# Shorter reciprocal square roots for every norm of a two-block fp32 kernel

## The chip, the cores and the metric

The kernel runs on one core of one Trainium2 chip, as one program. The metric is the device time of a run in microseconds; three runs of the kernel before are known. A further execution was taken by the hardware profiler, and every row shown here comes from that one.

## The reference

Two blocks in sequence, all in fp32, on 256 tokens of width 1024. The first has two layers; x (256 tokens) and a context xc (256 tokens, updated in layer 0 only) go through one set of weights:

```python
h = _rmsnorm(x, p["norm_g"]) * (1.0 + scale[:, None, :]) + shift[:, None, :]
hp = h @ p["w_in"]
...
y = jax.nn.silu(_layernorm(y, p["conv_ln_g"], p["conv_ln_b"]))
return y @ p["w_pw"] + p["b_pw"]
...
y = jnp.concatenate([attn, conv, four, sgu], axis=-1) * jax.nn.silu(hp[..., GATE_OFF:])
return y @ p["w_out"]
```

scale, shift and gate come from a product with w_ada. The attention has an rmsnorm on its query and key parts, the spatial gating (sgu) a layer norm. The result is rmsnorm(x, final_g). The second block has two layers of three steps, each with a norm before and behind it:

```python
x = x + 0.5 * rmsnorm(swiglu(rmsnorm(x, g[0]), ...), g[1])
x = x + rmsnorm(token_mixer(rmsnorm(x, g[2]), ...), g[3])
x = x + 0.5 * rmsnorm(swiglu(rmsnorm(x, g[4]), ...), g[5])
```

Each of these norms needs 1/sqrt of a mean square or variance for every token.

## The kernel before

Tokens lie on the 128 partitions: x is two tiles (t = 0, 1; x_80 and x_81 in the orders below), the context two more (t = 2, 3). An fp32 product is made as three fp32r products of high and low parts: ACT rounds a weight (`whi`, line 216 by its helper), DVE takes the rest (`wlo`, line 221), and PE runs whi*hi, whi*lo and wlo*hi (line 230; transposes are line 234). Weights and the chunks of w_ada come in over SP's queue as 512 KB tiles (`raw`, `ada`; line 330) into a few shared buffers, so that a fetch starts when an older tile has been consumed: a raw by its wlo on DVE, an ada chunk by its two `adaj` instructions on DVE, which multiply it with the condition and sum.

The order of all instructions is written when the program is built, by a planner (`Sched`). It keeps a clock for every engine, adds a cost for every instruction it issues (DVE: 0.07 us plus 0.00104 per element plus an extra; 0.13 between dependent instructions of one engine, 0.22 between engines), and starts side jobs, such as a conv's layer norm (`conv_out`), an ada chunk or a norm, when its clocks say that their inputs are there. A different cost anywhere can so change the order of everything behind it. The instruction streams themselves are static: an engine takes its instructions in that order, and waits where an input is late.

Stages of the first block, by layer: norm and modulation (`modulate`), the products with w_in (`u`), attention (`mla`), conv (31 `acc` steps per tile half on DVE), Fourier, sgu, the gate product (`u` of 256 columns), then for each branch `y` is multiplied (`fac`), transposed (`tpy`, into `yT`), and w_out is applied (`yo`), and x is updated. `conv_out` transposes acc (`tpc`), makes the layer norm from it (`bn`, `mv`, `rwl`, the root, `lnb`, then `ln` on ACT), transposes ln (`tpc` again), applies Silu or Tanh (`cs`, in layer 1 also `cv`), multiplies with w_pw (`pw`), and adds the row (`fac<-pw`). `norms` of the second block ends with x<-u_post,rs_y,x and the transposes of x for the next step (`tpx`).

The root is `rsqrt` (lines 372 to 386): a seed from the bits (rs_y, an integer operation on w), half of w negated (rs_h), then three steps y = (y*y*h + 1.5)*y. For width 1 a step is two instructions, for width 2 or 4 three. It is called by `rms` (norms, prenorm, the final norm; width 1), `modulate` (1), `layernorm` (1), `mla` (2, or 1 for keys alone), `attn_b` (4) and `First.start` (4).

Of the kernel before, what the change touches and what calls it, by code (L numbers as in the profile page):

```python
# [8 lines left out]
F32 = mybir.dt.float32  # L9
F32R = mybir.dt.float32r  # L10
I32 = mybir.dt.int32
AF = mybir.ActivationFunctionType
ALU = mybir.AluOpType
PSUM = bass.MemoryType.PSUM
P = 128
# [353 lines left out]

def rsqrt(S, ch, pool, w, n, tag):

    y = pool.tile([P, n], F32, tag=tag + "y", name="rs_y", bufs=4)
    h = pool.tile([P, n], F32, tag=tag + "h", name="rs_h")
    t = pool.tile([P, n], F32, tag=tag + "t", name="rs_t")
    S.dve(ch, n, "tensor_scalar", y.bitcast(I32), w.bitcast(I32), -0.5, float(0x5F3759DF), op0=ALU.mult, op1=ALU.add)
    S.dve(ch, n, "tensor_scalar", h, w, -0.5, None, op0=ALU.mult)
    for _ in range(3):
        if n == 1:  # L380
            S.dve(ch, n, "scalar_tensor_tensor", t, y, h, y, op0=ALU.mult, op1=ALU.mult, x=0.06)
        else:
            S.dve(ch, n, "tensor_tensor", t, y, y, op=ALU.mult)
            S.dve(ch, n, "tensor_tensor", t, t, h, op=ALU.mult)
        S.dve(ch, n, "scalar_tensor_tensor", y, t, 1.5, y, op0=ALU.add, op1=ALU.mult)
    return y


class Second:
# [57 lines left out]
    def rms(self, ch, ss, eps=D * EPS):  # L447

        w = self.small.tile([P, 1], F32, tag="rw", name="rw")
        self.S.dve(ch, 1, "scalar_tensor_tensor", w, ss[:, 0:1], eps, ss[:, 1:2], op0=ALU.add, op1=ALU.add)  # L450
        return rsqrt(self.S, ch, self.small, w, 1, "r")
# [413 lines left out]
    def attn_b(self, t, l, M, ev):  # L865
# [37 lines left out]
        for b in range(2):  # L903
# [7 lines left out]
        S.dve(ch, 256, "tensor_reduce", ss, sq, axis=mybir.AxisListType.X, op=ALU.add)  # L911
        S.dve(ch, 4, "tensor_scalar", ss, ss, 64 * EPS, None, op0=ALU.add)
        r = rsqrt(S, ch, small, ss, NB, "rb")
        S.dve(ch, 256, "scalar_tensor_tensor", o, o, 8.0 * (1.0 - LAM_INIT[l]), r.unsqueeze(2).to_broadcast([P, NB, 64]),
              op0=ALU.mult, op1=ALU.mult)
# [50 lines left out]
class First:  # L966
# [169 lines left out]
    def start(self):  # L1136
# [53 lines left out]
        w = self.small.tile([P, 4], F32, tag="rw4", name="rw4", bufs=1)  # L1190
        S.dve(cx, 4, "scalar_tensor_tensor", w, ss[:, :, 0], EPS, ss[:, :, 1], op0=ALU.add, op1=ALU.add)
        r = rsqrt(S, cx, self.small, w, 4, "r4")
        dg = [self.w2([P, P], f"diag{t}") for t in range(4)]
        for t in range(4):
# [662 lines left out]
def build(tc, a, wst, widths, n1, tab, ident, cols, rows, lamp, out):  # L1857
    nc = tc.nc
    with ExitStack() as ctx:
        def pool(name, bufs, **k):  # L1860
            return ctx.enter_context(tc.tile_pool(name=name, bufs=bufs, **k))


        pool("pad", 1).tile([P, PADS[0] // 4], F32, name="pad")
        wp, hp, work, rawp, cp = pool("wp", WBUFS), pool("hp", 2), pool("work", 2), pool("rawp", RAWB), pool("const", 1)
        small, psA = pool("small", 2), pool("psA", 1, space=PSUM)

        class PS:
            def tile(self, shape, dt, tag, name):
                return psA.tile(shape, dt, tag=tag, name=name, bufs={"ps": 6, "tp": 2}[tag])  # L1870

        X = [cp.tile([P, D], F32, name=f"x{t}") for t in range(2)]
        ones = cp.tile([P, P], F32, name="ones")
        nc.gpsimd.memset(ones, 1.0)
        idn = cp.tile([P, P], F32, name="ident")
        nc.gpsimd.dma_start(idn, ident)
        cl = cp.tile([P, cols.shape[1]], F32, name="cols")
        nc.gpsimd.dma_start(cl, cols)
        lp = cp.tile([P, 128], F32, name="subln")
        st = Stream(tc, wst, widths, rawp, wp, WBUFS, RAWB)  # L1880
        S = Sched(tc, st, LEAD)
        ps = PS()
        one = ExitStack()
        p1 = one.enter_context(tc.tile_pool(name="first", bufs=1, reuse_waits="tile"))
        first = First(tc, S, X, cl, idn, ones, ps, work, small, hp, p1, a, [0, n1 // 2])
        second = Second(tc, S, X, cl, rows, idn, lp, ones, out, ps, work, small, hp)
        first.end = second.first
        left = [0, 1]

        def main(t):  # L1890
            yield from first.main(t)
            left.remove(t)
            if not left:
                assert all(x[1].__name__ == "prenorm" for x in S.sides), S.sides
                one.close()
                p2 = ctx.enter_context(tc.tile_pool(name="second", bufs=1, reuse_waits="tile"))
                second.open(p2, tab)
                second.lambdas(lamp[:, :256])
                st.widen(st.alloc(p2, WMORE), WMORE)
                st.rawb = RAWB  # L1900
            yield from second.main(t)

        first.consts()
        S.spawn(first.start())
        st.widen(lambda i: [first.s4([P, 1024], f"w{n}{i}", F32R) for n in range(2)], WX[0], WX[1], WX[2])
        mains = {t: main(t) if t < 2 else first.main(t) for t in range(4)}
        nc.gpsimd.dma_start(lp, lamp[:, 256:].to_broadcast([P, 128]))
        S.run(mains)
# [37 lines left out]
```

## Time and profile before

| | us |
|---|---|
| median of three runs | 1448.87 (1445.61, 1448.87, 1448.91) |
| the profiled execution | 1447.77 |
| its span | 1446.0 |
| PE busy in the span | 1403.1 |
| DVE busy | 1002.7 |
| ACT busy | 765.8 |

The span runs from the first to the last recorded event of the profiled execution; the run's own time is 1.8 us longer. Busy times are of instructions and may overlap on an engine, since the next one can start before the last has ended. The first block takes from 0 to about 440 us, the second the rest.

### The profile page before, as it was taken

How to read it: one execution, taken by the hardware profiler on the slowest of the kernel's cores; microseconds unless marked ns; L12 is line 12 of the kernel's file. 1: busy time of each engine (PE TensorE's matmuls, PEld its weight loads, DVE VectorE, ACT ScalarE, POOL GpSimd, SP SyncE). 2: the span in 40 equal slices, each digit the busy share in tenths (PEclk: the TensorE clock that was granted, in tenths of full speed). 3: DMA queues.
4: the chain of work that ended last, by engine and by line, in shares of the span. 5: the costliest groups of instructions: out<-in, count | busy, mean ns of one | idle time of the engine just before them, and what ended most of it. 6: DMA issues, size and time to landing. Idle time of an engine off the chain costs nothing.

```text
span 1446.0 us, 19092 instructions
## 1 busy us (share of the span) xinstructions
PE 1403.1 (97%) x6766; PEld 1134.5 (78%) x6766; DVE 1002.7 (69%) x2175; ACT 765.8 (53%) x1348; POOL 30.0 (2%) x46
## 2 busy tenths in 40 slices
PE   7999997999999999999999999999999999999997
PEld 4778886777877888777878888788887778788886
DVE  4899978779787555587886555765555878865554
ACT  4465533576565444567655444554445676554442
POOL 1000000000000000000000000000000000000000
PEclk9999999999999999999999999999999999999999
DMA  8751455333456555653446566566566534466551
GB/s 304 238 172 59 128 192 162 123 124 121 159 189 209 186 188 188 190 186 121 139 139 204 189 180 186 173 193 187 188 189 189 182 125 134 143 200 186 185 186 58
DMA packets 69088, 245.64 MB, mean 170 GB/s; under 512 B 7841, under 2 KB 8097, under 8 KB 68865
## 3 DMA queue, kind: packets, MB, share of 16 engines
q1 hardware_dynamic: 66384, 235.11, 51.1%
q0 software_dynamic: 2176, 8.79, 1.8%
q8 instruction: 53, 0.87, 0.2%
q10 hardware_dynamic: 432, 0.53, 0.1%
q14 instruction: 43, 0.34, 0.1%
HBM read 243.35 MB, written 1.05 MB: 169 GB/s over the span
## 4 chain that ended last, share of the span: by engine, by line
PE 79%; DVE 11%; DMA 4%; ACT 3%; issue 2%; SPq 0%; DVEq 0%; ACTq 0%
PE u L230 37%; PE y L230 18%; PE m L230 9%; DMA raw<-in_wst_dram 3%; PE yo L230 3%; DVE adaj L221 2%; DVE wlo L221 2%; PE av L230 2%; PE tpg L234 2%; DVE acc L221 1%; ACT whi L216 1%; PE tpp L234 1%; DMA ada<-in_adan_dram 1%; PE sc L230 1%; ACT f L216 1%
## 5 line engine op out<-in xcount | busy, mean ns | idle before, releaser
L221 DVE TENSOR_TENSOR wlo<-raw,whi 128x1024 fp32r<-128x1024 f32 (+1 forms) x380 | 459.2, 1211 | 341.8 <-ACT whi L216 339.4
L216 ACT CAST whi<-raw 128x1024 fp32r<-128x1024 f32 (+1 forms) x380 | 395.3, 1042 | 386.7 <-PE u L230 228.5
L230 PE MATMUL u<-whi,h_hi 128*128 128x512 f32 x704 | 281.2, 400 | 1.1 <-ACT h_hi L216 1.1
L230 PE MATMUL u<-whi,h_lo 128*128 128x512 f32 x704 | 275.0, 391 | 0.6 <-DVE h_lo L221 0.6
L230 PE MATMUL u<-wlo,h_hi 128*128 128x512 f32 x704 | 275.5, 392 | 0.0
L230 PE MATMUL y<-whi,g 128*128 128x512 f32 x704 | 218.3, 390 | 0.5 <-ACT g L216 0.5
L230 PEld LDWEIGHTS y<-whi,g 128*128 128x128 f32 x704 | 132.0, 188 | 28.8 <-ACT g L216 0.8
L230 PEld LDWEIGHTS u<-wlo,h_hi 128*128 128x128 f32 x704 | 132.1, 188 | 27.7
L230 PEld LDWEIGHTS u<-whi,h_lo 128*128 128x128 f32 x704 | 132.5, 188 | 27.1 <-DVE h_lo L221 2.5
L230 PEld LDWEIGHTS u<-whi,h_hi 128*128 128x128 f32 x704 | 132.2, 188 | 26.4 <-ACT h_hi L216 1.7
L230 PE MATMUL y<-wlo,g 128*128 128x512 f32 x352 | 137.3, 390 | 0.0
L230 PE MATMUL u<-whi,hhi 128*128 128x512 f32 (+2 forms) x256 | 98.7, 388 | 0.4 <-ACT whi L216 0.3
L221 DVE CUSTOM_DVE_ANT_0 adaj<-ada,cbc 128x1024 bf16<-128x1024 f32 x76 | 90.6, 1221 | 8.7 <-DMA ada<-in_ada_dram 8.6
L230 PE MATMUL u<-wlo,hhi 128*128 128x512 f32 (+2 forms) x256 | 94.4, 372 | 0.4 <-DVE wlo L221 0.4
L230 PE MATMUL u<-whi,hlo 128*128 128x512 f32 (+2 forms) x256 | 94.8, 372 | 0.0
L230 PE MATMUL m<-whi,h_hi 128*128 128x512 f32 x192 | 79.0, 415 | 0.4 <-ACT h_hi L216 0.4
L230 PEld LDWEIGHTS y<-wlo,g 128*128 128x128 f32 x352 | 66.1, 188 | 14.3
L230 PE MATMUL m<-wlo,h_hi 128*128 128x512 f32 x192 | 75.5, 395 | 0.0
L230 PE MATMUL m<-whi,h_lo 128*128 128x512 f32 x192 | 75.3, 394 | 0.0
L221 DVE SCALAR_TENSOR_TENSOR acc<-glu,cw,acc 128x512 f32<-128x512 f32 (+1 forms) x120 | 70.8, 613 | 0.0
L230 PEld LDWEIGHTS u<-whi,hhi 128*128 128x128 f32 x256 | 48.2, 189 | 8.3 <-issue 1.9
L230 PEld LDWEIGHTS u<-wlo,hhi 128*128 128x128 f32 x256 | 48.2, 188 | 8.0 <-DVE wlo L221 1.2
(294 smaller groups left out, 1961.6 us busy)
## 6 DMA issues: line engine op xcount, KB each, us to landing
raw<-in_wst_dram SPq DMA_DIRECT2D x376, 512.0 KB, 3.6
ada<-in_ada_dram SPq DMA_DIRECT2D x42, 512.0 KB, 4.3
grow<-in_rows_dram POOLq DMA_DIRECT2D x10, 512.0 KB, 5.1
raw<-in_wst_dram SPq DMA_DIRECT2D x8, 416.0 KB, 3.1
ada<-in_adan_dram SPq DMA_DIRECT2D x6, 512.0 KB, 5.3
raw<-in_wst_dram SPq DMA_DIRECT2D x8, 256.0 KB, 2.8
tab<-in_tab_dram POOLq DMA_DIRECT2D x1, 1536.0 KB, 8.4
x<-in_x_dram SPq DMA_DIRECT2D x2, 512.0 KB, 5.4
```

Source lines behind the costliest of these rows:

```text
L216: ins = getattr(self.nc.scalar, fn)(*a, **k)
L221: ins = getattr(self.nc.vector, fn)(*a, **k)
L230: self.nc.tensor.matmul(*a, **k)
L234: self.nc.tensor.transpose(out, in_, ident)
```

## The change

`rsqrt` makes two steps instead of three: one of third order, y = ((t + H1)*t + H0)*y with t = y*w*y, and one of second order with scaled constants, y = (t + N0)*y. The seed's constant is another, the signs are folded into the constants, and h is not needed. For width 1 the instructions go from 8 to 6, for the others from 11 to 8. An assertion when the first block's buffers are closed allows one more kind of side job to be open.

```diff
@@ -369,20 +369,30 @@
+SEED, H1, H0, N0 = -552954042.0, -2.0555939659688196, 1.8980594831935855, -1.8898815769682833
 def rsqrt(S, ch, pool, w, n, tag):
     y = pool.tile([P, n], F32, tag=tag + "y", name="rs_y", bufs=4)
-    h = pool.tile([P, n], F32, tag=tag + "h", name="rs_h")
     t = pool.tile([P, n], F32, tag=tag + "t", name="rs_t")
-    S.dve(ch, n, "tensor_scalar", y.bitcast(I32), w.bitcast(I32), -0.5, float(0x5F3759DF), op0=ALU.mult, op1=ALU.add)
-    S.dve(ch, n, "tensor_scalar", h, w, -0.5, None, op0=ALU.mult)
-    for _ in range(3):
+    p = pool.tile([P, n], F32, tag=tag + "h", name="rs_p")
+    def square():
         if n == 1:
-            S.dve(ch, n, "scalar_tensor_tensor", t, y, h, y, op0=ALU.mult, op1=ALU.mult, x=0.06)
+            S.dve(ch, n, "scalar_tensor_tensor", t, y, w, y, op0=ALU.mult, op1=ALU.mult, x=0.06)
         else:
             S.dve(ch, n, "tensor_tensor", t, y, y, op=ALU.mult)
-            S.dve(ch, n, "tensor_tensor", t, t, h, op=ALU.mult)
-        S.dve(ch, n, "scalar_tensor_tensor", y, t, 1.5, y, op0=ALU.add, op1=ALU.mult)
+            S.dve(ch, n, "tensor_tensor", t, t, w, op=ALU.mult)
+    S.dve(ch, n, "tensor_scalar", y.bitcast(I32), w.bitcast(I32), -0.5, SEED, op0=ALU.mult, op1=ALU.add)
+    square()
+    S.dve(ch, n, "scalar_tensor_tensor", p, t, H1, t, op0=ALU.add, op1=ALU.mult)
+    S.dve(ch, n, "scalar_tensor_tensor", y, p, H0, y, op0=ALU.add, op1=ALU.mult)
+    square()
+    S.dve(ch, n, "scalar_tensor_tensor", y, t, N0, y, op0=ALU.add, op1=ALU.mult)
     return y
@@ -1891,7 +1901,7 @@
             yield from first.main(t)
             left.remove(t)
             if not left:
-                assert all(x[1].__name__ == "prenorm" for x in S.sides), S.sides
+                assert all(x[1].__name__ in ("prenorm", "swiglu") for x in S.sides), S.sides
                 one.close()
                 p2 = ctx.enter_context(tc.tile_pool(name="second", bufs=1, reuse_waits="tile"))
                 second.open(p2, tab)
```

The planner's costs of the root change with it, and so does the order. On DVE there are 2035 rows of the order before and 1910 now; the numbers of PE, ACT, POOL and SP instructions are the same, their order is not: about a thousand rows of PE move, nearly all in the first block.

PE, output stage of layer 0. u is the gate product's last part (its name has a number), tpc<-ident,acc and tpc<-ident,ln the conv's transposes, yo the product with w_out. Before:

```order
L234 MATMUL tpc<-ident,acc 128x128 x2
L230 MATMUL yo_2466<-whi_2259,yT_2281 128x512
L234 MATMUL tpc<-ident,acc 128x128 x2
L230 MATMUL yo_2466<-wlo_2260,yT_2280 128x512
L230 MATMUL yo_2466<-whi_2259,yT_2280 128x512
L230 MATMUL yo_2466<-whi_2259,yT_2281 128x512
L230 MATMUL yo_2466<-wlo_2260,yT_2280 128x512
L234 MATMUL tpc_2473<-ident,ln 128x128 x2
L234 MATMUL tpc_2491<-ident,ln 128x128 x2
L230 MATMUL pw<-pw,cs 128x256 x4
L234 MATMUL tpc_2521<-ident,ln 128x128 x2
L234 MATMUL tpc_2539<-ident,ln 128x128 x2
```

and now:

```order
L230 MATMUL u_2293<-wlo_2081,hhi 128x256
L234 MATMUL tpy<-ident,y_1417 128x128 x2
L234 MATMUL tpc_2345<-ident,ln 128x128 x2
L234 MATMUL tpc_2351<-ident,ln 128x128 x2
L230 MATMUL pw<-pw,cs 128x256 x4
L234 MATMUL tpc_2369<-ident,ln 128x128 x2
L234 MATMUL tpc_2381<-ident,ln 128x128 x2
L230 MATMUL pw<-pw,cs 128x256 x2
L234 MATMUL tpy<-ident,y_1226 128x128 x2
L230 MATMUL pw<-pw,cs 128x256 x2
L234 MATMUL tpy<-ident,y_1226 128x128 x4
L230 MATMUL yo_2410<-whi_2302,yT_1741 128x512
```

The conv's transposes of acc and ln and the pw product stood behind dozens of yo; now the transposes of acc stand further up, amid the gate product, and those of ln and the whole pw product stand between the gate product and the first yo.

DVE, the same place: ada_04 to ada_06 are chunks of w_ada of layer 1, y_1271 (before) and y_1226 (now) the branch that the transposes behind the gate product need. Before:

```order
L221 ISA adaj,ada_115<-ada_04_2112,cbc_117 128x1024
L221 ISA ada_115 128x1
L221 ISA adaj,ada_115<-ada_04_2112,cbc_118 128x1024
L221 ISA ada_115 128x1
L221 ISA adaj,ada_115<-ada_05_2142,cbc_117 128x1024
L221 ISA ada_115 128x1
L221 ISA adaj,ada_115<-ada_05_2142,cbc_118 128x1024
L221 ISA ada_115 128x1
L221 TENSOR_TENSOR y_1271<-y_1271,fac 128x256 x2
L221 TENSOR_TENSOR wlo_2236<-raw_2067,whi_2235 128x1024
L221 ISA adaj,ada_115<-ada_06_2165,cbc_117 128x1024
L221 ISA ada_115 128x1
```

and now:

```order
L221 SCALAR_TENSOR_TENSOR rs_y<-rs_t,rs_y 128x1 x2
L221 SCALAR_TENSOR_TENSOR lnb<-mv,rs_y 128x1 x2
L221 ISA adaj,ada_115<-ada_04_2095,cbc_117 128x1024
L221 ISA ada_115 128x1
L221 ISA adaj,ada_115<-ada_04_2095,cbc_118 128x1024
L221 ISA ada_115 128x1
L221 TENSOR_TENSOR yT_2020<-tpy,yT_2019 128x2x128
L221 ISA adaj,ada_115<-ada_05_2116,cbc_117 128x1024
L221 ISA ada_115 128x1
L221 ISA adaj,ada_115<-ada_05_2116,cbc_118 128x1024
L221 ISA ada_115 128x1
L221 TENSOR_TENSOR y_1226<-y_1226,fac 128x256 x2
```

Before, the conv's layer norms (rs_y, lnb) come some twenty rows behind ada_06; now they come ahead of ada_04, and ada_05 stands ahead of y, ada_06 behind its first pair.

PE, the boundary behind the first mixer of the second block: tpx transposes x_80 for the next unit, tpm transposes o_b, a part of the second token tile's attention. Before:

```order
L230 MATMUL y_1_7103<-whi_6952,m_hi 128x512
L230 MATMUL y_1_7103<-whi_6952,m_lo 128x512
L230 MATMUL y_1_7103<-wlo_6953,m_hi 128x512
L234 MATMUL tpm<-ident,o_b 128x128 x2
L234 MATMUL tpx<-ident,x_80 128x128 x4
L230 MATMUL y_0_7102<-whi_6979,m_hi 128x512
L230 MATMUL y_1_7103<-whi_6979,m_hi 128x512
L234 MATMUL tpx<-ident,x_80 128x128 x4
```

and now:

```order
L234 MATMUL tpm<-ident,o_b 128x128 x2
L230 MATMUL y_1_7027<-whi_6879,m_hi 128x512
L230 MATMUL y_1_7027<-whi_6879,m_lo 128x512
L230 MATMUL y_1_7027<-wlo_6880,m_hi 128x512
L230 MATMUL y_0_7026<-whi_6906,m_hi 128x512
L230 MATMUL y_1_7027<-whi_6906,m_hi 128x512
L234 MATMUL tpx<-ident,x_80 128x128 x8
```

The first four transposes of x_80 move two y matmuls down, to the other four; tpm moves three up.

## Rows read from the trace of the kernel before

**Rows 1.** The page's first part: busy time, share and instructions of each engine.

```profile
PE 1403.1 (97%) x6766; PEld 1134.5 (78%) x6766; DVE 1002.7 (69%) x2175; ACT 765.8 (53%) x1348; POOL 30.0 (2%) x46
```

**Rows 2.** Busy time by stretch; then PE's granted clock, DMA share, GB/s.

```profile
210.00:240.00 30.00, 26.46 (x147) 22.43 (x145) 25.06 (x64) 9.00 (x16) 0.31 (x1) 0.94 0.65 211
240.00:270.00 30.00, 25.61 (x120) 20.27 (x119) 21.39 (x58) 13.72 (x31) 0.00 (x0) 0.94 0.47 149
760.00:914.00 154.00, 154.00 (x694) 125.45 (x693) 83.21 (x97) 72.41 (x96) 0.00 (x0) 1.00 0.61 191
```

**Rows 3.** PE's waits: total us, times, longest us.

```profile
PE tpc L234 <- ACT ln L216: 4.0, 1, 4.0
PE tpx L234 <- DVE x L221: 4.0, 5, 0.9
PE tpy L234 <- DVE y L221: 3.5, 1, 3.5
...
PE tpy L234 <- ACT cv L216: 1.6, 1, 1.6
```

**Rows 4.** Instructions that write rs_y: ns min/median/max, first and last start, forms.

```profile
L221 DVE SCALAR_TENSOR_TENSOR rs_y<-rs_t,rs_y x165: 136/158/168, 14.4 to 1441.4; 128x1 f32<-128x1 f32 x132, 128x2 f32<-128x2 f32 x18, 128x4 f32<-128x4 f32 x15
```

**Rows 5.** Timeline of DVE, one root of width 1: start us, us, line.

```profile
269.95 0.15 DVE L221 TENSOR_SCALAR rs_y<-rw 128x1 int32<-128x1 int32 x1
270.02 0.14 DVE L221 TENSOR_SCALAR rs_h<-rw 128x1 f32<-128x1 f32 x1
270.20 0.22 DVE L221 SCALAR_TENSOR_TENSOR rs_t<-rs_y,rs_h 128x1 f32<-128x1 f32 x1
270.46 0.16 DVE L221 SCALAR_TENSOR_TENSOR rs_y<-rs_t,rs_y 128x1 f32<-128x1 f32 x1
...
271.55 0.49 DVE L221 TENSOR_SCALAR xn<-x,rs_y 128x512 f32<-128x512 f32 x1
```

**Rows 6.** Timeline of DVE at the end of the span.

```profile
1441.64 1.42 DVE L221 SCALAR_TENSOR_TENSOR x<-u_post,rs_y,x 128x512 f32<-128x512 f32 x2
```

**Rows 7.** Timeline of PE and DVE at boundaries of the second block.

```profile
612.95 1.29 PE L234 MATMUL tpx<-ident,x 128*128 128x128 f32 x8 [0.74 <-DVE x L221]
...
740.18 0.63 PE L234 MATMUL tpx<-ident,x 128*128 128x128 f32 x4 [0.90 <-DVE x L221]
...
941.01 1.42 DVE L221 SCALAR_TENSOR_TENSOR x<-u_post,rs_y,x 128x512 f32<-128x512 f32 x2
...
941.90 0.63 PE L234 MATMUL tpx<-ident,x 128*128 128x128 f32 x4
```

**Rows 8.** Timeline of PE in the output stage of layer 0.

```profile
217.23 1.09 PE L230 MATMUL yo<-whi,yT 128*128 128x512 f32 x4
...
234.72 0.62 PE L230 MATMUL yo<-whi,yT 128*128 128x512 f32 x2
...
245.14 1.14 PE L234 MATMUL tpc<-ident,ln 128*128 128x128 f32 x4 [4.03 <-ACT ln L216]
...
284.78 0.39 PE L230 MATMUL u<-whi,hhi 128*128 128x512 f32 x1
```

**Rows 9.** Timeline of DVE in the same stage.

```profile
212.12 1.23 DVE L221 CUSTOM_DVE_ANT_0 adaj<-ada,cbc 128x1024 bf16<-128x1024 f32 x1
...
239.94 0.76 DVE L221 BATCH_NORM_STATS2 bn<-tpc 128x6 f32<-128x256 f32 x2
...
240.70 1.20 DVE L221 TENSOR_TENSOR wlo<-raw,whi 128x1024 fp32r<-128x1024 f32 x1
...
243.98 0.16 DVE L221 SCALAR_TENSOR_TENSOR lnb<-mv,rs_y 128x1 f32<-128x1 f32 x1
```

**Rows 10.** Timeline of ACT in the same stage.

```profile
243.58 1.04 ACT L216 CAST whi<-raw 128x1024 fp32r<-128x1024 f32 x1 [2.96 <-DMA raw<-in_wst_dram]
...
245.62 1.51 ACT L216 ACTIVATE cs<-tpc,cols 128x128 f32<-128x128 f32 x4
```

**Rows 11.** The page's DMA issues: count, KB each, median us to landing.

```profile
raw<-in_wst_dram SPq DMA_DIRECT2D x376, 512.0 KB, 3.6
```

## Prediction

> **What bounds the kernel now.** Read the page's first part first: TensorE (PE) is busy 97% of the span and VectorE (DVE) 69% [rows 1]. Then the stretches: in the second block PE is busy 154.00 us of 154 while it does a feed-forward unit, but in 210:240 and 240:270, the output stage of layer 0 of the first block, it is busy only 26.46 and 25.61 of 30, and there the granted clock averages 0.94 [rows 2]. So DVE work that is removed is worth nothing by itself over most of the span; it counts only where PE waits for a chain that a root lies in. The list of PE's waits says where: ln, the conv branch's layer norm in layer 0 (one wait of 4.0), x after the second block's norms (five waits, 4.0 together), cv, the conv branch of layer 1 (1.6); and y, which has no root before it but stands in DVE's queue (one wait of 3.5) [rows 3]. That is 13.1 us out of 1446, and no gain from these waits can be larger.
>
> **How much a root shortens.** The row of the last step counts the calls: 132, 18 and 15 instructions of widths 1, 2 and 4 over three steps are 44, 6 and 5 calls [rows 4]. The undisturbed chain shows their pace: seed at 269.95, h 0.07 behind it (the two don't wait for each other), t at 270.20, y 0.26 behind t, the result's reader at 271.55, so 1.60 us, and the three steps, from 270.20 on, take 0.45 each [rows 5]. The change takes h and one step away (8 instructions become 6 for width 1, 11 become 8 otherwise) and puts one dependent instruction (p) in. From t on, the chain loses 0.45 and gains 0.20, and the seed's reader comes some 0.05 sooner: about **-0.3 us** per call of width 1; for the others a step of three dependent instructions goes (0.6) and one comes (0.2): about -0.45. Since 121 instructions of some 0.15 to 0.22 us disappear, DVE's busy time should fall by about 20 us from 1002.7; I cost that at nothing, since PE covers it.
>
> [...]
>
> **The end.** The last norm's chain ends in the write of x at 1441.64 [rows 6], and after it only the output's transfer follows. Nothing covers it: **-0.3**.
>
> **Five boundaries of the second block.** Each of the waits of rows 7 at tpx ends with the x that a root scaled. After the feed-forward units (612.95 and two like it, 0.74 each) the transposes of x_80 stand behind the same matmuls as before, so each wait shrinks by 0.3: -0.9. After the mixers (740.18 and one like it, 0.90 each) the planner now puts the first four transposes two matmuls (0.45) later: 0.90 - 0.3 - 0.45 leaves 0.15. But it puts tpm<-ident,o_b three matmuls (0.68) earlier, behind a width-4 root that is 0.45 shorter; a new wait of 0.2 is due. Net -0.5 each, -1.0. The five places of x_81 move one to three matmuls (0.23 each) earlier against a chain 0.3 shorter. The tightest is 941.90: the first half of x is written at 941.01 + 0.71, and the transposes will stand 0.68 earlier with x only 0.3 earlier: +0.4, the others within 0.1 [rows 7]. Sum **-1.4**; bounds -4.0 (all five waits go) and +1.2 (nine matmuls of 0.23 earlier, paid in full, less the 0.9).
>
> **The output stage of layer 0** is where the changed costs turn the order over. Before, PE ends the gate matmuls at 217.23, runs w_out's matmuls (yo), waits twice among them and starts layer 1 at 284.78 [rows 8]. In the new order the conv's transposes stand amid the gate matmuls, and the pw product and its transposes are all done before the first yo. So I replay the chain that releases the first yo, by the durations of now. DVE ends adaj_17 at 212.12 + 1.23 = 213.35. A pair of layer norms takes 4.2 from bn at 239.94 to the end of lnb, with one 1.20 wlo inside, so 3.0, and 2.7 with the shorter roots [rows 9]: 216.05. The second pair has two wlo inside and stands behind ACT's two ln and two casts (about 1.0 each): 221.9. Now ada_04, 05 and 06 stand ahead of all else, 6 x 1.23 = 7.4, with a yT and a pair of y between: 230. Only then is a raw buffer free for the second of the two casts that ACT has ahead of the second cs; now too ACT sat 2.96 at such a cast [rows 10]. A fetch takes 3.6 [rows 11], the cast 1.04, half of the cs 0.8 [rows 10], pw and tpy some 1.3: the first yo at about 237. From there PE has 192 yo at 0.23 (two in 0.62, one in 0.39) [rows 8], 44.2, 38 transposes of about 0.12, 4.6, and the half-clock start: after a wait PE runs slowly, as the clock of 0.94 over 30 us shows, which is 1.8 us lost [rows 2]. End: 237.3 + 44.2 + 4.6 + 1.8 = 287.9 against 284.78, **+3** in round numbers. The cost arises because PE, which now waits 3.5 and 4.0 us there with yo before, between and behind, will wait some 7 and then 9 us with no yo to fill. Bounds: if the raw buffer comes early the second wait of 8.9 goes, -5.9; if the fetch is late by as much as the one that held ACT's cast for 2.96 [rows 10], +6. I take +3, what the rows' durations give. Two weights of the gate matmuls (w16, w22) are also needed a little sooner than they are converted; PE's waits for them, a microsecond each, are covered by the 7 us wait behind, and cost that again if it is not there.
>
> **Layer 1 of the first block.** The conv's transposes move thirty places up, amid the gate matmuls, and the wait for cv (1.6) [rows 3] should mostly go: **-1.0**, between -1.6 (it goes) and +2 (the planner's new order makes one like layer 0's on a small scale).
>
> **Sum.** -0.3 - 1.4 + 3 - 1 = +0.3 on the profiled execution's 1447.77 (its span is 1446.0): **1448.1**. The median of the three runs shown is 1448.87, and they spread from 1445.61; the profiled one lies between.
>
> **Rivals.**
> (A) Faster, 1439.2: the first stage keeps pace. If DVE comes into it earlier (it was nearly full from 90 us on, and its roots there are shorter) or the freed buffers come in another order, ada_06 doesn't hold the raw fetch, the second wait of 8.9 is gone, and the two waits of 3.5 and 4.0 are not replaced: 1448.1 - 8.9. For it: the conv's chain now starts under the gate matmuls, where PE has work. Against it: three ada chunks stand on DVE ahead of the fetch in the new order, whatever starts when.
> (B) Slower, 1455.5: the same place at its upper bound. Price: +6 there, +2 in layer 1, nothing won at the boundaries, the end -0.3: 1447.77 + 7.7. It decides from the point where the second cs can't start before 235: then PE is idle more than 9 us in one piece. For it: the order rows, and a cast that already waits 2.96 for its transfer; against it: the fetch may find free queues.
> (C) The new order nets nothing and only the shorter chains show: 1447.77 - 0.3 - 1.4 = 1446.1.
> (D) That the roots don't get shorter would need p's step to run slower than y's; same form, same width, so I give it nothing of its own.
>
> **How the numbers follow.** A measurement of this kernel tells 0.3% (4.35 us) from no change, so "same" is 1444.5 to 1453.2. Chances: forecast 0.38, A 0.27, B 0.20, C 0.15. Of the forecast 0.02 falls under 1444.5 and 0.05 over 1453.2, of C 0.03 under. Faster 0.27 + 0.02 + 0.03 = 0.32, same 0.43, slower 0.20 + 0.05 = 0.25. The range goes to A's and B's values, 1440 to 1455.5; the forecast's own is 1444 to 1453.
>
> **What would show it.** DVE's busy time near 982 and 2050 instructions; the chain from seed to reader 1.3 us; the waits at tpx 2 to 2.6 us in total; the last write of x 1.3 us behind its seed. In layer 0: two long waits of PE, at tpc or pw<-cs, before the first yo near 237, with the granted clock under 0.9 in 210:240; layer 1's first u near 288. Wrong if yo starts before 232 (then A), or if PE's waits have moved elsewhere in the first block, to weights for instance. The planner has many places to shift work that I have not replayed.

## The result, and the profile after

The changed kernel took 1458.91 us (median of four runs, 1457.96 to 1461.29) against 1448.53 for the kernel before in the same comparison: a ratio of 1.0079, with a 95% interval from 1.0064 to 1.0093. It is slower by 10.4 us, above the range that was given. The profiled execution of it has a span of 1456.2 us, 10.2 more than before [rows 1]:

```profile
PE 1408.2 (97%) x6766; PEld 1138.2 (78%) x6766; DVE 993.2 (68%) x2054; ACT 767.6 (53%) x1348; POOL 30.1 (2%) x46
```

DVE lost its 121 instructions (2175 to 2054), and 9.5 us of busy time, not 20. Cut at four moments that both traces have, the 10.2 us lie here:

| from, to | before | after | difference | forecast |
|---|---|---|---|---|
| start to the end of adaj_17 on DVE | 213.35 | 220.77 | +7.4 | 0 |
| from there to layer 1's first u on PE | 71.4 | 78.1 | +6.7 | +3 |
| from there to the second block's first m on PE | 330.2 | 329.1 | -1.2 | -1.3 |
| from there to the end | 831.0 | 828.3 | -2.7 | -1.4 |

m is the first matmul of the second block's first mixer; its first feed-forward unit, and the first of the five boundaries of the forecast (-0.3), lie ahead of it.

**What went as forecast: the chain and the second block.** The last root, on DVE's timeline (start, duration), stands against [rows 5] and [rows 6]:

```profile
1450.52 0.15 DVE L221 TENSOR_SCALAR rs_y<-rw 128x1 int32<-128x1 int32 x1
1450.70 0.22 DVE L221 SCALAR_TENSOR_TENSOR rs_t<-rs_y,rw 128x1 f32<-128x1 f32 x1
1450.96 0.16 DVE L221 SCALAR_TENSOR_TENSOR rs_p<-rs_t 128x1 f32<-128x1 f32 x1
...
1451.80 1.41 DVE L221 SCALAR_TENSOR_TENSOR x<-u_post,rs_y,x 128x512 f32<-128x512 f32 x2
```

From seed to reader it takes 1.28 us instead of 1.60: 0.32 less, with the square and p where they were expected; the dependent instructions of one element start 0.18 to 0.26 us apart (1450.52, 1450.70, 1450.96). The boundaries, on PE's timeline, against [rows 7]:

```profile
625.86 1.29 PE L234 MATMUL tpx<-ident,x 128*128 128x128 f32 x8 [0.49 <-DVE x L221]
```

```profile
752.48 0.63 PE L234 MATMUL tpx<-ident,x 128*128 128x128 f32 x4
753.39 0.66 PE L234 MATMUL tpx<-ident,x 128*128 128x128 f32 x4 [0.28 <-DVE m_lo L221]
```

The wait behind the feed-forward unit is 0.49 instead of 0.74, and the one behind the mixer, 0.90 before, is gone, with 0.28 behind it for m_lo.

**What did not: the first block.** PE's waits (total, times, longest), against [rows 3]:

```profile
PE pw L230 <- ACT cs L216: 6.0, 2, 5.1
PE tpy L234 <- ACT ln L216: 3.0, 1, 3.0
PE tpx L234 <- ACT f L216: 2.7, 1, 2.7
PE av L230 <- ACT pT L216: 2.4, 1, 2.4
PE dft L230 <- ACT dftz L216: 2.2, 2, 1.7
...
PE tpx L234 <- DVE x L221: 1.5, 3, 0.5
...
PE tpy L234 <- ACT cv L216: 0.3, 1, 0.3
```

Two rows of before that are not among those:

```profile
PE tpx L234 <- ACT f L216: 1.4, 3, 0.6
...
PE dft L230 <- ACT dftz L216: 0.8, 1, 0.8
```

The wait for x fell from 4.0 to 1.5 and that for cv from 1.6 to 0.3, as forecast. The two long ones of the output stage (3.5 and 4.0) have others in their place (pw for cs, 5.1 at most; tpy for ln, 3.0), av for pT (2.4) is new, and the waits of tpx for f and of dft for dftz have grown, from 1.4 in three to 2.7 in one and from 0.8 to 2.2. By stretches (PE's busy time first, then its granted clock after the other engines), 60:205 before and after, then 120:150 before and after, then two stretches after against [rows 2]:

```profile
60.00:205.00 145.00, 144.73 (x743) 118.16 (x742) 138.17 (x347) 79.18 (x192) 0.53 (x1) 1.00 0.44 141
```

```profile
60.00:205.00 145.00, 139.13 (x694) 111.53 (x693) 134.60 (x319) 77.91 (x186) 0.00 (x0) 0.99 0.40 130
```

```profile
120.00:150.00 30.00, 30.00 (x166) 24.69 (x166) 29.37 (x75) 17.05 (x43) 0.00 (x0) 1.00 0.22 71
```

```profile
120.00:150.00 30.00, 25.94 (x133) 20.09 (x132) 27.62 (x67) 14.36 (x35) 0.00 (x0) 0.94 0.20 71
210.00:240.00 30.00, 22.71 (x142) 19.45 (x140) 24.73 (x78) 11.21 (x23) 1.07 (x2) 0.89 0.62 207
240.00:270.00 30.00, 26.95 (x126) 22.17 (x126) 18.84 (x36) 10.37 (x25) 0.00 (x0) 0.89 0.40 136
```

PE did nothing for 0.3 of the 145 us of 60:205 before and for 5.9 now. In 120:150 it was busy all of the 30 us; now it is 25.94, and the clock there is 0.94. In the two stretches of the output stage the clock is 0.89 instead of 0.94; behind the wait of 5.11 at 243.05, shown below, it was 0.50 (243:246), then 1.00 (247.6:252).

**The output stage of layer 0** on DVE, against [rows 9]:

```profile
219.55 1.22 DVE L221 CUSTOM_DVE_ANT_0 adaj<-ada,cbc 128x1024 bf16<-128x1024 f32 x1
...
223.21 0.28 DVE L221 SCALAR_TENSOR_TENSOR lnb<-mv,rs_y 128x1 f32<-128x1 f32 x2
...
229.30 0.28 DVE L221 SCALAR_TENSOR_TENSOR lnb<-mv,rs_y 128x1 f32<-128x1 f32 x2
...
236.22 1.22 DVE L221 CUSTOM_DVE_ANT_0 adaj<-ada,cbc 128x1024 bf16<-128x1024 f32 x1
```

SP's queue and ACT behind it, against [rows 10]:

```profile
237.48 0.33 SPq L330 DMA_DIRECT2D raw<-in_wst_dram  x1
```

```profile
241.59 1.04 ACT L216 CAST whi<-raw 128x1024 fp32r<-128x1024 f32 x1 [1.79 <-DMA raw<-in_wst_dram]
242.54 1.50 ACT L216 ACTIVATE cs<-tpc,cols 128x128 f32<-128x128 f32 x4
```

and PE, against [rows 8]:

```profile
230.11 0.47 PE L234 MATMUL tpy<-ident,y 128*128 128x128 f32 x2 [2.98 <-ACT ln L216]
...
233.89 3.61 PE L230 MATMUL pw<-pw,cs 128*128 128x256 f32 x8 [0.94 <-ACT cs L216]
...
243.05 2.08 PE L230 MATMUL pw<-pw,cs 128*128 128x256 f32 x4 [5.11 <-ACT cs L216]
...
247.60 0.70 PE L230 MATMUL yo<-whi,yT 128*128 128x512 f32 x2
...
298.85 0.80 PE L230 MATMUL u<-whi,hhi 128*128 128x512 f32 x1 [0.20 <-ACT hhi L216]
```

This is the replay, link by link, 7.4 us later: the second lnb, then six adaj instead of the conv's row, the fetch at 237.48 just behind the last of them (236.22 + 1.22), the cast at 241.59 waiting for it, the second cs behind the cast, and PE idle for 5.11 at 243.05. The first yo starts at 247.60, against 237.3 in the forecast.

**Ahead of it, in the conv stretch,** DVE, ACT and PE after the change:

```profile
130.76 0.41 DVE L221 BATCH_NORM_STATS2 bn<-u 128x6 f32<-128x256 f32 x1
...
135.18 0.15 DVE L221 SCALAR_TENSOR_TENSOR rs_p<-rs_t 128x1 f32<-128x1 f32 x1
135.25 0.75 DVE L221 SCALAR_TENSOR_TENSOR acc<-glu,cw,acc 128x512 f32<-128x512 f32 x1
...
139.05 0.15 DVE L221 SCALAR_TENSOR_TENSOR lnb<-mv,rs_y 128x1 f32<-128x1 f32 x1
```

```profile
139.29 0.56 ACT L216 ACTIVATE ln<-u,lnb,rs_y 128x256 f32<-128x256 f32 x1 [0.43 <-DVE lnb L221]
...
148.98 0.56 ACT L216 ACTIVATE ln<-u,lnb,rs_y 128x256 f32<-128x256 f32 x1 [6.19 <-DVE lnb L221]
```

```profile
140.84 0.71 PE L230 MATMUL av<-V,pT 128*128 128x128 f32 x4 [2.39 <-ACT pT L216]
...
150.07 1.13 PE L230 MATMUL dft<-dftz,cdsd 128*128 128x256 f32 x4 [1.66 <-ACT dftz L216]
```

The third layer norm of sgu runs on DVE from 130.76 to 139.05. Almost every one of its ten dependent steps has a conv step (acc, 0.74 us of duration), a maximum or a weight's wlo behind it, so the steps take as long as the nine instructions between them. In ACT's order ln stands ahead of the softmax's p and of pT, and av on PE waits 2.39 for that pT. Not all of the 2.39 is the layer norm's: ln keeps ACT for 0.9 (0.43 of waiting, 0.47 until p starts), and ahead of it ACT was at a cast that had waited 0.97 for its fetch. At the fourth layer norm ACT waits 6.19, and dft on PE waits 1.66 for the dftz behind it. Before the change the same layer norm took no less on DVE (118.19 to 129.28), but its end lay ten microseconds earlier, and ACT did not wait for it:

```profile
118.19 0.43 DVE L221 BATCH_NORM_STATS2 bn<-u 128x6 f32<-128x256 f32 x1
```

```profile
129.13 0.15 DVE L221 SCALAR_TENSOR_TENSOR lnb<-mv,rs_y 128x1 f32<-128x1 f32 x1
```

```profile
130.34 0.60 ACT L216 ACTIVATE ln<-u,lnb,rs_y 128x256 f32<-128x256 f32 x1
```

In the order before, 32 conv steps stand ahead of that layer norm's lnb, and 39 now.

The fourth layer norm shows that a late chain is only half of it. Before the change ACT waited nearly as long for it, 5.89, with pT and dftz behind it, and PE did not wait, because it had other work: it ran 21 matmuls of u between 142 and 150 us. ACT and PE before:

```profile
146.08 0.57 ACT L216 ACTIVATE ln<-u,lnb,rs_y 128x256 f32<-128x256 f32 x1 [5.89 <-DVE lnb L221]
```

```profile
143.48 0.39 PE L230 MATMUL u<-whi,hlo 128*128 128x512 f32 x1
```

In the new order the matmuls of u come sooner: the last one starts at 138.07, and there is none between 139 and 150. The new order made the third layer norm late and also took away what PE had to do meanwhile.

### The profile page after: what moved, and what is told of

The parts are those of the page before. It is cut to its first block, busy times and chain, and to the rows that moved or that the text cites. A ratio compares the mean times of both kernels' runs of the same rounds, so it can differ in the third digit from the quotient of the medians.

```text
span 1456.2 us, 18965 instructions
## 1 busy us (share of the span) xinstructions
PE 1408.2 (97%) x6766; PEld 1138.2 (78%) x6766; DVE 993.2 (68%) x2054; ACT 767.6 (53%) x1348; POOL 30.1 (2%) x46
## 4 chain that ended last, share of the span: by engine, by line
PE 81%; DVE 9%; ACT 4%; DMA 4%; issue 2%; SPq 0%; DVEq 0%; ACTq 0%
PE u L230 37%; PE y L230 18%; PE m L230 9%; PE yo L230 4%; DMA raw<-in_wst_dram 3%; DVE adaj L221 2%; PE av L230 2%; ACT whi L216 1%; PE tpg L234 1%; DVE wlo L221 1%; PE tpp L234 1%; PE sc L230 1%; DVE acc L221 1%; DMA ada<-in_adan_dram 1%; ACT f L216 1%
```

## Experiments

Eleven kernels ran, each against the kernel before on the same chip. Two theories stood at the start: the order that comes from the smaller costs does the harm, or the shorter instruction sequence does.

**1. Roots and costs apart.** The planner's charge was separated from the instruction: `charge` is what `S.dve` adds to the planner's clock for one DVE instruction.

```diff
-    S.dve(ch, n, "scalar_tensor_tensor", p, t, H1, t, op0=ALU.add, op1=ALU.mult)
+    S.nc.vector.scalar_tensor_tensor(p, t, H1, t, op0=ALU.add, op1=ALU.mult)
...
+    charge()
+    charge()
+    for _ in range(3):
+        square_cost()
+        charge()
     return y
```

> The changed roots, but the planner is charged what the old ones cost, so that its clocks and the order of the DMA fetches stay those of before. Theory P (the loss of 10 us comes from the order that the planner writes from the smaller costs): 1445.5 to 1447.5, since only the shorter chains show: about 0.3 us less at each of five waits for x in the second block and at the end. Rival R (the loss comes with the shorter instruction sequence itself, whatever the planner is told): 1455 or more.

Measured: 1452.45 us, ratio 1.0028 (1.0015 to 1.0041), between the two theories. The second block behaved as foreseen (828.3 us from its first m to the end), but that m came at 622.78 instead of 615.01. The planner is charged what it was before, and SP's 461 fetches come in the same order in both traces; still at least 130 of PE's 6766 matmuls, compared by name, stand elsewhere (at least 409 after the change). So the planner's clocks alone do not fix the order; that the instructions are placed once more when the program is built, and fall out otherwise with two fewer in each root, is the likely reason, which no run isolates. Here too the third layer norm stands behind 38 conv steps, and av waits 1.41 for pT. Of the 7.8 us that are lost up to the first m, 4.2 lie ahead of layer 1's first u (288.96 instead of 284.78) and 3.6 behind it, where PE waits for a weight's whi:

```profile
307.50 0.72 PE L230 MATMUL u<-whi,hhi 128*128 128x416 f32 x1 [3.94 <-ACT whi L216]
```

The converse has the old instructions and is charged what the new root costs:

> The old roots, but the planner is charged what the new ones cost. Theory P: 1458 to 1463, the loss of the change and 1 to 3 us more for the longer chains. Rival R: 1447 to 1450.

Measured: 1460.89, ratio 1.0086 (1.0068 to 1.0104); first m at 628.74, 830.8 us from there. The order does the harm without the shorter roots, as theory P said.

**2. From which call on.** The charge is the new one until a flag that conv_out sets ahead of its first layer norm.

```diff
 def conv_out(self, l, t, acc, at):
...
+        CALLS[1] += 1
         z = self.layernorm(ch, tp[:, :256], 256)
...
+    if CALLS[1] == 0:
```

> The changed roots; the planner is charged their new cost up to the first layer norm of a conv in layer 0, the old cost from there on. The order of TensorE is that of the change up to the first w_out matmuls of layer 0. Theory P with the loss made in layer 0 (7 us before the output stage, 6 in it): layer 1's first u near 298, and 1454 to 1461 in all. Rival (the loss depends on the costs of the later part too): layer 1's first u under 290, and 1451 or less.

Measured: 1462.10, ratio 1.0089 (1.0072 to 1.0106); layer 1's first u at 298.15, first m at 631.60. The u came where theory P had it, the time 1.1 over its range. The new costs of the early calls are enough for the 13 to 14 us up to layer 1 (with short roots and old costs throughout it was 4.2); with the old costs behind them the way from there to the first m took 333.5 us, 4.4 more than with the change, not less.

**3. The late fetch.** One raw buffer more, which the planner is not told of; the padding tiles shrink to make room.

```diff
-PADS = (1920, 608, 704)
+PADS = (64, 608, 64)
...
-pool("rawp", RAWB)
+pool("rawp", RAWB + 1)
```

> The changed kernel with one more raw buffer (padding is given up for it), which the planner is not told of. Theory F (a weight's fetch that waits behind ada chunks for a buffer makes the wait of 5.1 us for the second cs): that wait falls under 2 us, and the time by 3 to 4, to 1454.5 to 1456. Rival L (VectorE enters the stage 7 us late, and its queue sets the end whatever is fetched): the wait moves to another releaser and the time stays within 1457.5 to 1460.

Measured: 1458.50, ratio 1.0065 (1.0050 to 1.0080), the changed kernel's time within the intervals. SP, ACT and PE show why:

```profile
234.64 0.33 SPq L330 DMA_DIRECT2D raw<-in_wst_dram  x1
```

```profile
237.68 1.04 ACT L216 CAST whi<-raw 128x1024 fp32r<-128x1024 f32 x1 [5.98 <-DMA raw<-in_wst_dram]
...
239.17 1.51 ACT L216 ACTIVATE cs<-tpc,cols 128x128 f32<-128x128 f32 x4
```

```profile
239.69 1.65 PE L230 MATMUL pw<-pw,cs 128*128 128x256 f32 x3 [6.61 <-ACT cs L216]
...
244.08 1.13 PE L230 MATMUL pw<-pw,cs 128*128 128x256 f32 x4 [0.33 <-ACT cs L216]
...
246.72 0.71 PE L230 MATMUL yo<-whi,yT 128*128 128x512 f32 x2
```

The fetch is issued 2.8 us sooner (234.64), and the second cs no longer holds PE (0.33). But the order moved too: the cast of the fetch before (237.68) now stands ahead of the gate's fac and of the first cs, and PE waits 6.61 for that. The link from fetch to cast to cs is borne out; what it costs isn't, because the order moved with the buffer. The time is rival L's; its reason is not shown by this run.

**4. The two places, one constant each.** CONV bounds how far the conv may run ahead on DVE, ADA when the ada chunks are forced. For these constants the order says what the first block will have: 38 conv steps ahead of the third layer norm and more than 60 yo ahead of the conv's ln (CONV 2.5); 28 steps and no yo (ADA 24); 29 steps and 54 yo (both).

```diff
-CONV = 3
+CONV = 2.5
```

> The changed kernel with the planner's CONV at 2.5 instead of 3. In this order the transposes of the conv's ln stand behind some 60 yo again, as before the change, but the third layer norm of sgu on VectorE still comes behind 38 conv steps (32 before the change). Theory of two places (about 5 us are lost ahead of the output stage through that late layer norm, 4 to 5 in the stage through the missing yo): av still waits 2 us or more for pT near 140, and the stage from the first gate matmul of 256 columns to layer 1's first u takes 80.5 us as before, so 1452.5 to 1455.5. Rival (the early loss is all that counts, the stage only passes it on): 1457 to 1460.

Measured: 1450.48, ratio 1.0012 (0.9995 to 1.0028): 8.4 us of the 10.4 are back, more than expected. PE in the stage:

```profile
249.15 0.69 PE L234 MATMUL tpy<-ident,y 128*128 128x128 f32 x2 [3.44 <-ACT ln L216]
...
293.04 1.12 PE L234 MATMUL tpx<-ident,xn 128*128 128x128 f32 x4 [3.16 <-ACT f L216]
```

First yo at 225.90 and layer 1 at 293.89, 5.0 sooner than after the change; av still waits for pT, 1.43 and once 1.49. In the stage PE still waits for ln (3.44) and f (3.16), where after the change its longest wait was 5.11. But the gate product already begins 2.7 sooner (211.11, 213.79 after the change), and from there to layer 1's first u it takes 82.8 us, where 80.5 was expected, 80.5 was measured before and 85.1 after the change. So only 2.3 of the 5.0 us are the stage's, and that the yo back in the stage take away most of the loss is not shown.

```diff
-ADA = (0.3,25,0.75,1.5)
+ADA = (0.3,24,0.75,1.5)
```

> The changed kernel with the planner's ADA deadline at 24 instead of 25. In this order the third layer norm of sgu comes behind 28 conv steps, earlier than before the change, but no yo stands ahead of the conv's ln. Theory of two places: no wait of av or dft above 1 us near 140 to 150, gate matmuls begin about 5 us sooner than with the change; the output stage still takes some 85 us; 1452 to 1455.5. Rival (only the output stage counts): 1457 to 1460, with the wait of PE made longer there.

Measured: 1459.44, ratio 1.0075 (1.0060 to 1.0090). This half of the theory missed; the time is the rival's. The wait of av at 140 is gone, but others are there instead, 3.46 for a weight's whi at 84.99 and

```profile
151.44 2.07 PE L230 MATMUL dft<-dftz,cdsd 128*128 128x256 f32 x4 [3.69 <-ACT dftz L216]
```

and in the output stage PE waits 9.19 and 6.56 for ln. The gate product begins at 215.98, not sooner than with the change.

> The changed kernel with both constants: CONV 2.5 and ADA 24. Third layer norm of sgu behind 29 conv steps, conv's ln behind 54 to 66 yo. Theory of two places: 1445 to 1449.5, the loss gone and the shorter chains of the second block left. Rival (each new order brings its own new waits of that size): anywhere from 1450 to 1458.

Measured (both diffs): 1453.43, ratio 1.0035 (1.0023 to 1.0047): neither the best nor the loss, and in the rival's range.

> The kernel before, with the same two constants and the old roots. Theory of two places: the order has its third layer norm at 29 and the conv's ln behind 72 yo, as good as before: 1446 to 1451. If it is faster than 1444, the constants win by themselves and the run with both places shows them and not the repair. Rival (each new order brings its own waits): over 1451.

Measured: 1462.25, ratio 1.0093 (1.0078 to 1.0108). The old roots, with an order that has neither place later than it was before the change (29 conv steps instead of 32, 72 yo both times), lose 14 us, with waits in other places (2.12 for dftz at 123.33 is a third):

```profile
84.05 0.79 PE L230 MATMUL u<-whi,hhi 128*128 128x512 f32 x1 [3.14 <-ACT whi L216]
...
297.70 1.11 PE L234 MATMUL tpx<-ident,xn 128*128 128x128 f32 x4 [5.50 <-ACT f L216]
```

So the constants don't win by themselves; and these two places are not enough to judge an order by.

**5. One block at a time.** The short root stands beside the old one under another name, and the methods of one block call it.

```diff
 class Second:
...
-        return rsqrt(self.S, ch, self.small, w, 1, "r")
+        return rsqrt_short(self.S, ch, self.small, w, 1, "r")
```

> The changed roots and their costs in the second block alone; the first block keeps the old roots, costs and order, instruction for instruction. Theory S (the shorter chains are worth 2.6 us in the second block, and the whole loss is the new order of the first): from the first m matmul of the second block to the end 828 to 829 us instead of 831.0, that matmul at 615 as before, and 1445 to 1446.5, a ratio of 0.998 to 0.9988 to the kernel before. Rival (the second block's shorter chains are given back at its own entry, where the order changes too): 1447.5 to 1449.

Measured over five rounds: **1445.19 us, ratio 0.9977 (0.9966 to 0.9988)**, faster than both kernels. In the traces PE's first 2149 matmuls, up to about 447 us, stand in the order of before; first m at 614.91, 828.4 us from there, and PE's waits for x are 1.5 us in three, 0.5 at most, as after the change. That the first m comes only 0.1 sooner hides two things. In this execution the first block, in the same order, ran 2.3 us ahead of the profiled one of before (the same matmul of u at 432.29 and 434.61); at the second block's entry that was lost again, as PE waited 1.75 for h_hi at 439.87 (0.87 before) and the seven matmuls of u from 441.41 on started 0.43 apart (0.23 before); the granted clock was 0.99 in 300:450 (1.00 before). So two executions of one order can differ by 2 us in the first block, and a difference of that size between two traces shows nothing there.

> The converse: changed roots and costs in the first block alone, with the change's order there; old roots and costs in the second block. Theory S: the first m matmul at 627 to 629, 830.7 to 831.2 us from there, and 1460.5 to 1462.5. Rival (part of the loss sits in the second block): under 1459.

Measured: 1459.86, ratio 1.0078 (1.0061 to 1.0094); first m at 626.29, 830.9 us from there. Theory S holds in kind, though the m comes 0.7 and the time 0.6 sooner than it expected; nothing points to a part of the loss in the second block.

> The changed roots with the planner charged the old costs, and CONV at 2.5. The third layer norm of sgu stands behind 32 conv steps, as before the change, and all of the conv's ln behind 72 yo. Theory of two places: the first m matmul at 615 to 617, and 1444 to 1447. Theory O (two places are not enough to tell an order: every order other than the one before brought 7 to 17 us of waits of its own to the first block): first m at 620 or later, and 1450 to 1460.

Measured: 1453.78, ratio 1.0038 (1.0026 to 1.0049); first m at 626.05. Theory O, and the end of the theory of two places as a way to find a good order: the layer norm stands where it was, the yo are there, and the waits are elsewhere, 3.95 for a weight's whi at 309.38 among them. Nearly half of what is lost lies behind layer 1's first u (290.84, 6.1 later than before; the first m 11.0 later).

**The runs together.** The time splits cleanly at the second block's first m:

| kernel | roots, costs in the first block | first m | from there to the end |
|---|---|---|---|
| before | old, old | 615.01 | 831.0 |
| the change | new, new | 627.92 | 828.3 |
| new roots, old costs | new, old | 622.78 | 828.3 |
| old roots, new costs | old, new | 628.74 | 830.8 |
| second block alone | old, old | 614.91 | 828.4 |
| first block alone | new, new | 626.29 | 830.9 |

To the right the roots alone decide: 828.1 to 828.8 in all nine runs with short roots in the second block, 830.8 to 831.0 in the four with old ones. To the left the order decides: the eleven kernels with another order of the first block (the change among them) gave 622.1 to 631.6.

## Why the prediction was wrong

- **The chain, the end, the boundaries: right.** 0.32 us per root of width 1 for 0.3. The end and the four boundaries behind the first m gave -2.7 for -1.4, since the transposes of x_81, which were to cost 0.5, show no wait, and the mixers' waits of 0.90 went, with 0.28 behind them. From the first m on PE's waits fell from 5.9 to 4.0 us and the time behind its last matmul by 0.3; about 0.5 of the 2.7 is in no wait.
- **DVE's busy time: wrong, without effect.** It fell by 9.5 us, not 20. The durations were taken as if nothing overlapped. In the conv stretch the next instruction starts 0.07 us after a root's step of 0.15 (135.18, 135.25), so a step taken away there frees 0.07; over the whole program 9.5 / 121 gives 0.08 for each. The order has no part in it: DVE is busy 993.3 us with the short roots at old costs and 1002.9 with the old roots at new costs.
- **The output stage: the mechanism right, the size short.** The term was +3; it measured +6.7. The order of events is the replay's. Two links were mis-sized: the fetch took 4.1 to the cast instead of 3.6, and "pw and tpy some 1.3" took 4.55 (243.05 to 247.60). In the run with a fifth buffer the same matmuls took 2.64 (244.08 to 246.72), and in the kernel before 2.63 (250.25 to 252.88) at a granted clock of 1.00; here the granted clock was 0.52 (243:247.6), behind a wait of 5.11, and four pw took 2.08 instead of 1.13. So about 1.9 us, an estimate from these runs, are the clock's, and 1.3 were counted too few. The sum has 1.8 us for the half-clock start. Before, the clock was 0.50 in 221.9:224.5, behind the wait of 3.54, and 0.56 in 245.14:249, behind that of 4.03, but 1.00 in 441.31:444, behind one of 0.87 for h_hi. By the prediction's working the clock of 0.89 over the 60 us of 210:270 is 6.6 us, where 0.94 was 3.6 before.
- **The step that failed** is the sentence "DVE ends adaj_17 at 212.12 + 1.23 = 213.35". It takes the new stage's entry from the old order's timeline. That entry came 7.4 us later, and this is the larger part of the loss. The conv stretch ahead of it (60:205), where PE had waited 0.3 us before, had waits of 5.9 us, and a slower clock behind them: 0.94 over the 30 us of 120:150, which is 1.8 us by the prediction's own working. 5.6 and 1.8 make up the 7.4; no run takes the one without the other. The prediction knew that DVE was nearly full there and drew only the hope of an earlier start from it (rival A). It looked for what a shorter chain frees, not for what a chain that starts later holds up. The start to adaj_17 had no term in the sum, so no bound of it was in the range. The prediction's last sign of being wrong, PE's waits moved elsewhere in the first block, is the one that came.
- **Rival B** named the right sign and one of the two places, 1455.5; with the missing 7.4 it would have been past the measured time. Its own sign, PE idle more than 9 us in one piece, did not come (5.11 at most), and its +2 in layer 1 and nothing at the boundaries were wrong. A chance of 0.25 for slower was too little: between "order changed in a thousand rows" and "time unchanged" there was nothing in the rows to hold the time.
- **Layer 1: right, in part by luck**, -1.2 for -1.3 with the boundary in it. The wait for cv went as forecast (1.6 to 0.3). But in the other kernels with a moved first block the same way, from layer 1's first u to the first m, took 323.9 to 335.2 us, so an agreement within 0.1 is partly luck.

What stays open is which moved row costs how much in the conv stretch. Every attempt to mend one wait there moved others, as the runs of groups 3 and 4 show, and no run changes one wait alone. That the moved order of the first block makes the loss is shown; that the third layer norm or the matmuls of u taken away from 139 to 150 are its main part is read from the traces and not tested.

## What to carry to other kernels

Where a planner writes the order from its costs, a cheaper operation is two changes, the operation and a new order: try the operation with the order held, first where the order does not depend on it. Charging the planner the old cost did not hold it here; keeping the old operation in the block with the sensitive order did. Here the shorter root was worth 2.6 us in the block whose order hardly moved, and the moved order of the other block cost 12.9 (627.92 - 615.01). A stage replayed in a new order must be entered at the new order's own time; an order that runs full on two engines ahead of it is the first place to look.

## What the runs showed of the hardware

Where DVE was nearly full (busy 27.62 of the 30 us of 120:150), a dependent chain was slowed not by its own instructions but by about one other instruction of its queue per step: the same layer norm takes about 8 us amid conv steps (130.76 to 139.05), while two layer norms that hardly anything else disturbs take 2.8 together (220.70 to 223.49), and an undisturbed root is read 1.28 us behind its seed. A step taken away there freed 0.07 us of the engine (135.18, 135.25), and 0.08 as the mean of the program. ACT passed such a chain on: it did nothing for the 6.19 us up to 148.98 while work for PE stood behind the waiting ln. Whether PE paid for that hung here on what else its own order held: it waited 1.66 there, and not at all before the change, when ACT had idled 5.89 at the same place.
